# First stage in another order: 1/rms row later, norm of v ahead of its mixing adds, evictions and M6 of u ahead of S3 and A22, identity products before the first weights

## The chip, the cores and the metric

The kernel runs on one core of a Trainium2 chip. The metric is device microseconds (us) of one execution; less is better. Of the engines, PE (TensorE) does matrix products, DVE (VectorE) and ACT (ScalarE) do elementwise work, POOL (GpSimd) does little here, and SP (SyncE) issues nearly all DMAs. Each engine works through its own list of instructions in order; semaphores order the lists among each other. PE's results stand in PSUM banks, all else in SBUF or in HBM.

## What is computed

One decoder block on 1024 tokens of width 1024, in float32. Cut to what matters here:

```
h = rms_norm(x, g)                                   # x * rsqrt(mean(x^2) + eps) * g
rnn_x, rnn_gate, sgu_u, sgu_v, gate_a, gate_b = split(h @ w_in)
y_a = gelu(rnn_gate) * rg_lru(conv4(rnn_x))          # recurrence over the tokens
v   = layer_norm(gelu(sgu_v))                        # over all 1024 columns of v
y_b = gelu(sgu_u) * (tril(w_s) @ v + b_s)            # per chunk of 128 tokens, 8 groups
x  += (sigmoid(gate_a)*(y_a @ w_proj_a) + sigmoid(gate_b)*(y_b @ w_proj_b)) @ w_out
x  += (silu(g) * u) @ w_down,  [g|u] = rms_norm(x) @ w_gate_up
return rms_norm(x)
```

## The kernel before

Every product of two f32 matrices is made of three products of split operands: a value is written as hi + lo, and `mm3` issues hi·hi, hi·lo and lo·hi (lines 97, 98 and 99 in the profile). A split is two instructions: ACT writes hi (L93), then DVE subtracts to get lo (L94). Nearly every operand and every piece of a weight passes through this pair. A piece of a weight is 128x512, a part of an activation operand 128x1024 (`part`).

Only the first stage, about the first 200 us, is touched. It has four steps.

Step 1, `wv0`: the first half of the columns of v. x, already transposed in HBM (`xt`), is loaded by quarters (256 tokens) and split with the gain in it (`x_split`, L450 on ACT, L451 on DVE), and eight tiles of 128 tokens go through 24 products each into PSUM (`pv`). Beside this the untransposed x is loaded (`x_load`, tile `xn` with three buffers), squared and summed on ACT (L454), and 1/rms is computed in a chain of small DVE instructions (`rstd_early`, L382 to L391). `x_rms` then puts it on a diagonal `dg` (L463 ACT, L464 DVE), and `x_row` multiplies that by ones on PE (L473), which gives 1/rms as a row over the tokens. With it `scale_x` scales x in place, for the later products. gelu of v reads PSUM with 1/rms as the scale (`gelu_v0` L486, statistics L530).

Step 2, `wv1`: the other half of the columns, again eight tiles of 24 products. After each tile ACT applies gelu (L611) and DVE takes statistics (L612, L618); `v_norm` computes 1/std (L624, then the chain) and centres (L630, ACT); two tiles later `v_split` makes the split normalized v (`vn`, L636 ACT, L637 DVE) and `v_mix` multiplies it with the mixing weights `ws` (PE L647, L648), copies half the result (ACT L650), adds the other (DVE L651) and stores it to HBM (L652, tensor `mix_d`). In between `sums` and `sum_s4` build S1 to S4 out of the four blocks A11, A12, A21 and A22 of the scaled x, and `part` splits them.

Step 3: `u0` and `u1`, two column blocks of u. They are multiplied by a seven-product scheme (`wino`): M1, M2, M5, M6, M3, M7, M4 of 12 products each, whose left operands are A11, A12, S1, S2, S4, S3 and A22, and whose right operands (b11, b21, t1, t2, b22, t3, t4) are made from a 1 MB piece of a weight by DVE subtractions (L206 to L217) and splits. The two go in turn. M1, M6, M7 and M4 run into one PSUM tile, `p1`, so M6 can start only after M1 has been copied out (`post`, L233 on ACT), and M4 only after M7 has been added in (L243 on DVE). While step 3 starts, `post` is put off: its calls are kept in `postponed` and made after all of S3 and A22. Then the results of u are multiplied with the mixed v, which comes back from HBM (DVE L788, gelu L789 on ACT, DVE L791) and are stored.

Step 4: `r0`, a column block of rnn_x, in the same scheme; its result runs through the convolution (`xc`, L857 on ACT, L859 on DVE) and is split (`xs`), and the gate products `pgt` of PE wait for that. After `r0` the rest of the kernel follows in the same rhythm.

Steps 1, 2 and the start of 3 stand under `manual_schedule`: each engine's list there has the order in which the code is written. Behind it a list scheduler orders instructions by its own costs. The lines that it works on are the same, but what of the first part is left to it can be mixed in anywhere behind.

Of the kernel before, what the change touches and what calls it, by code (L numbers as in the profile page):

```python
# [51 lines left out]
def block_kernel(ctx: ExitStack, tc: tile.TileContext, a: dict, out: bass.AP):  # L52
# [139 lines left out]
    cur, postponed = {"misc": None}, []  # L192
# [29 lines left out]
    def wino(name, ops, c11, c21, c12, c22, c11_dst=None, order=STEADY):  # L222
# [28 lines left out]
        for m in order:  # L251
# [163 lines left out]


# [3 lines left out]
    H = [[slot(f"h{h}{kh}") for kh in range(2)] for h in range(2)]  # L420
    ops = {}
    with tc.tile_pool(name="phv", bufs=1) as wk:
        ws = wk.tile([P, GROUPS, 2, P], F32R, name="ws")
        shift = wk.tile([P, GROUPS, P], F32, name="shift")
# [8 lines left out]
        xn = {}  # L433
        a22 = []
        dgs = {}

        def xt_load(q, ks=slice(0, NK)):
            c = slice(2 * P * (q % 2), 2 * P * (q % 2 + 1))
            nc.sync.dma_start(F[q // 2][:, ks, c], a["xt"][q][:, ks])
# [13 lines left out]
        def squares(t):  # L453
            act.activation(xn[t], xn[t], AF.Square, accum_out=ssqs[:, t:t + 1])  # L454

        def x_rms(q):
# [3 lines left out]
            dg = wk.tile([P, 2, 2, P], F32R, name=f"dg{q}", tag="dg")  # L460
# [4 lines left out]
            dgs[q] = dg  # L465
# [91 lines left out]
        x_load(3)  # L557
        xt_load(3)
        x_load(4)
        x_rms(0)  # L560
        x_split(2)
        for t in range(2, NT):
            acc[t] = ps(f"pv0{t}")
            tm_half(acc[t], "wv0", H, t, range(NK), free=NK * (t == NT - 1))
            if t == 2:
                x_row(0)
# [37 lines left out]
        part("A11", block(0, 0, 1), 1)  # L604
# [755 lines left out]
```

## Time and profile before

| | |
|---|---|
| median of 3 runs | 1451.16 us (1450.82 to 1451.53) |
| profiled execution | 1452.88 us |
| its span from first to last instruction | 1451.2 us |
| mean granted clock of TensorE | 0.990 of full speed |
| PE busy | 1400.2 us, 96% of the span |
| DVE busy | 1098.3 us, 76% |
| ACT busy | 793.5 us, 55% |
| chain that ended last | PE 76%, DVE 11%, ACT 6%, DMA 4%, issue 2% |

The chain is followed back from the last instruction, at each step to what released it, so its shares say on which engine the end hangs. By the page's slices PE has its low ones at the start and around the span's tenth, and from there on it stands at 90% or more until the last slice; the granted clock is below full speed in the first four slices only. The steps in time: wv0 runs to 59 us, wv1 to 129 us, u0 and u1 to about 183 us, and r0 to 205 us.

### The profile page before, as it was taken

The numbers are of one execution on the slowest core, as the hardware profiler recorded it, in microseconds if no ns is written. First come the engines' busy times: TensorE is split into PE (matmuls) and PEld (weight loads), VectorE is DVE, ScalarE is ACT, GpSimd is POOL, SyncE is SP. The second block draws the span as 40 slices with busy tenths as digits, with TensorE's granted clock in tenths as the row PEclk, the third lists the DMA queues.
The fourth block names the chain that finished last, engine by engine and source line by source line (L and its number), as shares of the span: only waits on it lengthen the run. The fifth ranks groups of instructions, "written<-read, shape, count | busy, mean of one in ns | idle before, by whom it ended". The sixth has DMA issues, their size and how long they took to land.

```text
span 1451.2 us, 17181 instructions
## 1 busy us (share of the span) xinstructions
PE 1400.2 (96%) x6192; PEld 1153.3 (79%) x6192; DVE 1098.3 (76%) x1803; ACT 793.5 (55%) x1315; POOL 74.8 (5%) x59
## 2 busy tenths in 40 slices
PE   7998699999999999999999999999999999999997
PEld 5776587788888888778888788888888888888886
DVE  6878889988888878597855966666666665697585
ACT  6456668789888876262443633333333333444454
POOL 0000000000000000000000011111111111100000
PEclk9998899999999999999999999999999999999999
DMA  8412445632233367676531032222222226853342
GB/s 294 157 44 70 157 173 176 206 123 93 78 122 140 117 261 293 234 263 217 188 122 44 22 134 109 109 109 110 105 88 105 103 81 266 312 196 109 109 138 80
DMA packets 72821, 212.45 MB, mean 146 GB/s; under 512 B 6560, under 2 KB 20384, under 8 KB 60192
## 3 DMA queue, kind: packets, MB, share of 16 engines
q1 hardware_dynamic: 72592, 211.32, 40.8%
q8 instruction: 48, 0.79, 0.2%
q14 instruction: 37, 0.30, 0.1%
q10 hardware_dynamic: 144, 0.04, 0.0%
HBM read 148.68 MB, written 62.65 MB: 146 GB/s over the span
## 4 chain that ended last, share of the span: by engine, by line
PE 76%; DVE 11%; ACT 6%; DMA 4%; issue 2%; SPq 0%; DVEq 0%; ACTq 0%; POOL 0%; POOLq 0%
PE f_p L99 10%; PE f_p L97 10%; PE f_p L98 10%; PE d_M L98 5%; PE d_M L97 5%; PE d_M L99 5%; PE g_p L99 3%; PE g_p L98 3%; PE g_p L97 3%; PE r_p L99 2%; DMA sb<-sgb_d 2%; PE r_p L98 2%; PE r_p L97 2%; PE po L97 2%; PE po L99 2%; PE po L98 2%
## 5 line engine op out<-in xcount | busy, mean ns | idle before, releaser
L93 ACT ACTIVATE dl_M<-wraw 128x512 fp32r<-128x512 f32 x77 | 48.6, 631 | 104.8 <-PE d_M L99 89.8
L98 PE MATMUL d_M<-d_M,dl_M 128*128 128x512 f32 x264 | 102.8, 389 | 0.0
L97 PE MATMUL d_M<-d_M,dl_M 128*128 128x512 f32 x264 | 102.7, 389 | 0.0
L99 PE MATMUL d_M<-d_M,dl_M 128*128 128x512 f32 x264 | 102.7, 389 | 0.0
L93 ACT ACTIVATE f_t<-wraw 128x512 fp32r<-128x512 f32 x88 | 55.5, 630 | 83.8 <-PE f_p L99 71.4
L94 DVE TENSOR_TENSOR dl_M<-wraw,dl_M 128x512 fp32r<-128x512 f32 x77 | 54.0, 701 | 51.5 <-ACT dl_M L93 51.3
L94 DVE TENSOR_TENSOR f_t<-wraw,f_t 128x512 fp32r<-128x512 f32 x88 | 71.7, 815 | 23.7 <-ACT f_t L93 22.6
L97 PE MATMUL f_p<-m,f_b 128*128 128x512 f32 x176 | 69.2, 393 | 0.0
L98 PE MATMUL f_p<-m,f_b 128*128 128x512 f32 x176 | 69.0, 392 | 0.0
L99 PE MATMUL f_p<-m,f_b 128*128 128x512 f32 x176 | 69.0, 392 | 0.0
L98 PE MATMUL f_p<-m,f_t 128*128 128x512 f32 x176 | 68.5, 389 | 0.0
L99 PE MATMUL f_p<-f_S,f_t 128*128 128x512 f32 x176 | 68.5, 389 | 0.0
L97 PE MATMUL f_p<-f_S,f_t 128*128 128x512 f32 x176 | 68.5, 389 | 0.0
L99 PE MATMUL f_p<-m,f_t 128*128 128x512 f32 x176 | 68.5, 389 | 0.0
L97 PE MATMUL f_p<-m,f_t 128*128 128x512 f32 x176 | 68.5, 389 | 0.0
L98 PE MATMUL f_p<-f_S,f_t 128*128 128x512 f32 x176 | 68.5, 389 | 0.0
L93 ACT ACTIVATE f_b<-wraw 128x512 fp32r<-128x512 f32 x66 | 41.1, 626 | 36.8 <-PE f_p L99 31.6
L94 DVE TENSOR_TENSOR f_b<-wraw,f_b 128x512 fp32r<-128x512 f32 x66 | 45.3, 687 | 19.6 <-ACT f_b L93 18.9
L97 PE MATMUL pv<-wv,h 128*128 128x512 f32 x128 | 51.5, 403 | 7.8 <-ACT wv L93 7.8
L97 PEld LDWEIGHTS d_M<-d_M,dl_M 128*128 128x128 f32 x264 | 49.6, 188 | 10.4
L98 PEld LDWEIGHTS d_M<-d_M,dl_M 128*128 128x128 f32 x264 | 49.6, 188 | 10.3 <-DVE d_M L94 0.2
L99 PEld LDWEIGHTS d_M<-d_M,dl_M 128*128 128x128 f32 x264 | 49.6, 188 | 10.3
(504 smaller groups left out, 4213.0 us busy)
## 6 DMA issues: line engine op xcount, KB each, us to landing
wraw<-in_w_gu_dram SPq DMA_DIRECT2D x22, 1024.0 KB, 4.8
wd<-in_w_down_dram SPq DMA_DIRECT2D x11, 1024.0 KB, 9.4
wraw<-in_w_r_dram SPq DMA_DIRECT2D x8, 1024.0 KB, 6.1
wraw<-in_w_g_dram SPq DMA_DIRECT2D x8, 1024.0 KB, 4.8
wraw<-ffs_d SPq DMA_DIRECT2D x8, 1024.0 KB, 5.1
wraw<-ffa_d SPq DMA_DIRECT2D x6, 1024.0 KB, 6.1
xn<-in_x_dram SPq DMA_DIRECT2D x8, 512.0 KB, 6.2
wraw<-in_w_u_dram SPq DMA_DIRECT2D x4, 1024.0 KB, 5.3
```

Source lines behind the costliest of these rows:

```text
L93: act.activation(hi, src, AF.Copy)
L94: (eng or dve).tensor_sub(lo, src, hi.bitcast(F32))
L97: pe.matmul(o, lh, rh, start=start, stop=False, **kw)
L98: pe.matmul(o, lh, rl, start=False, stop=False, **kw)
L99: pe.matmul(o, ll, rh, start=False, stop=stop, **kw)
```

## The change

It writes the first stage in another order, and has to house some tiles elsewhere for it.

1. Start: the first 512 KB piece of transposed x is loaded as two of 256 KB (128 tokens each), and its splits are halved with it. Before the first real product PE gets 12 products of the 128x128 f32 identity with itself into a PSUM tile that nobody reads (`warm`).
2. 1/rms: `x_row` of each quarter comes one tile later; the diagonal (`x_diag`) is made after the next quarter's `x_split` instead of before it. The untransposed x has a slot of four tiles (`xn`) instead of three buffers, so its loads are issued earlier. A11 is split in wv1 instead of wv0, since it takes over that slot.
3. Norm of v: `v_norm` runs for the groups 0, 1+2, 3+4, 5+6, 7, right behind the statistics of its last tile. The additions of the mixed tile of two tiles before (`v_mixed`), which stood ahead of the norm, now stand behind it, and the centring (`v_centre`) behind those. S1's split comes one or more tiles later than its sum.
4. u: the PSUM copies and additions (`post`) are no longer put off until after S3 and A22: `take(2)` makes them two at a time in between, and four products of each u (M1, M2, M5, M6) instead of three are written out under `manual_schedule`. S3 and A22 are split after that. A22 is now scaled in place and copied by ACT (two instructions 128x1024, in tiles that the last stores of mixed v must have left) before its split. What the finished results of u trigger (`results`) is still called behind the manual part.

```diff
-    cur, postponed = {"misc": None}, []
+    cur, postponed = {"misc": None, "defer": False}, []
...
-            if cur["misc"] is None:
+            if cur["defer"]:
                 postponed.append(lambda m=m: post(m))
...
+    xn = slot("xn", (P, 4, D), F32)
     ops = {}
+    new_misc("misc1")
...
-            xn[t] = wk.tile([P, D], F32, name=f"xn{t}", tag="xn", bufs=3)
-            nc.sync.dma_start(xn[t], a["x"][ts(t), :])
...
+            nc.sync.dma_start(xn[:, t % 4], a["x"][ts(t), :])
...
             rstd_early(wk, ssqs[:, c], 1.0 / D, f"rx{q}", 2, rms[:, c])
-            dg = wk.tile([P, 2, 2, P], F32R, name=f"dg{q}", tag="dg")
+
+        def x_diag(q):
+
+            dg = dgs[q] = wk.tile([P, 2, 2, P], F32R, name=f"dg{q}", tag="vb", bufs=3)
...
-                y = F[h][:, k]
-                if h == 1 and k >= 4:
-                    if k % 2 == 0:
-                        a22.append(wk.tile([P, 2, HALF], F32, name=f"a22_{k}", tag="xn", bufs=3))
-                    y = a22[-1][:, k % 2]
-                dve.scalar_tensor_tensor(y, F[h][:, k], par("mix_g", k), R[h], ALU.mult, ALU.mult)
+                dve.scalar_tensor_tensor(F[h][:, k], F[h][:, k], par("mix_g", k), R[h], ALU.mult, ALU.mult)
...
-            s1 = wk.tile([P, 2, HALF], F32, name=f"xs{i}", tag="xn", bufs=3)
-            dve.tensor_add(s1, block(1, 0, i), a22[i])
-            part("S1", s1, i)
+            s1 = s1s[i] = wk.tile([P, 2, HALF], F32, name=f"xs{i}", tag="shift")
+            dve.tensor_add(s1, block(1, 0, i), block(1, 1, i))
...
-        xt_load(0, slice(0, 4))
+        first, second = slice(0, P), slice(P, 2 * P)
+        xt_load(0, slice(0, 4), first)
         start_loads(1)
+        xt_load(0, slice(0, 4), second)
         xt_load(0, slice(4, 8))
...
+        warm = ps("warm")
+        for _ in range(12):
+            pe.matmul(warm[:, :P], ident, ident, start=True, stop=True, skip_group_check=True)
...
             if t == 2:
-                x_row(0)
                 v0_done(0, acc[0])
...
             if t == 3:
+                x_row(0)
                 x_split(3)
+                x_diag(1)
...
-                part("A11", block(0, 0, 0), 0)
-                x_rms(3)
                 v0_done(6, acc[6])
             tick()
         x_row(3)
-        part("A11", block(0, 0, 1), 1)
...
+        group = {t: [t] if t in (0, NT - 1) else [t - (t + 1) % 2, t + t % 2] for t in range(NT)}
...
+            if 1 <= t < 3:
+                part("A11", block(0, 0, t - 1), t - 1)
+            if t == 2:
+                sums(0)
+            if t == 4:
+                part("S1", s1s[0], 0)
+                sums(1)
...
             v_stats(t, acc)
-            if t == NT - 1:
+            if t == group[t][-1]:
                 v_norm(t)
             if t > 1:
                 v_mix(t - 2)
-            if t in (1, 3, 5, 6):
-                v_norm(t)
+                v_mixed(t - 2)
+            if t == group[t][-1]:
+                v_centre(t)
             tick()
...
+        def take(n):
+            for fn in postponed[:n]:
+                fn()
+            del postponed[:n]
+
+        cur["defer"] = True
         v_split(6)
         head("u0")
         v_mix(6)
+        v_mixed(6)
         v_split(7)
         head("u1")
-        part("S2", block(0, 0, 0), 0)
+        take(2)
         head("u0")
         v_mix(7)
+        v_mixed(7)
+        part("S2", block(0, 0, 0), 0)
+        head("u1")
         part("S2", block(0, 0, 1), 1)
+        take(2)
+        head("u0")
         head("u1")
         part("S4", block(0, 1, 0), 0)
+        take(2)
+        part("S4", block(0, 1, 1), 1)
         head("u0")
-        part("S4", block(0, 1, 1), 1)
         head("u1")
-        for i in range(2):
-            part("S3", block(1, 0, i), i)
-        for i in range(2):
-            part("A22", a22[i], i)
...
+        take(2)
+        cur["defer"] = False
     ms.__exit__(None, None, None)
...
-        for fn in postponed:
+        for fn in results:
             fn()
-        postponed.clear()
+        results.clear()
+        for i in range(2):
+            part("S3", block(1, 0, i), i)
+        for i in range(2):
+            c = wk.tile([P, 2, HALF], F32, name=f"a22_{i}", tag="rr")
+            act.activation(c, block(1, 1, i), AF.Copy)
+            s1s[i] = c
+        for i in range(2):
+            part("A22", s1s[i], i)
```

The order in which the engines get this stands below at three places.

The first is DVE in wv1: `mv` and `rv` are the norm's tiles (L118 to L129 of the list), `mt` the additions of mixed v, `vn` the splits of normalized v. Before:

```order
L651 TENSOR_TENSOR mt10_849<-mt10_849,mx10_844 128x256
L651 TENSOR_TENSOR mt11_858<-mt11_858,mx11_853 128x256
L651 TENSOR_TENSOR mt12_867<-mt12_867,mx12_862 128x256
L651 TENSOR_TENSOR mt13_876<-mt13_876,mx13_871 128x256
L624 TENSOR_SCALAR mv2_771<-mv2_771 128x2
L382 TENSOR_SCALAR rv3_881<-mv2_771 128x2
L383 TENSOR_SCALAR rv3_881<-rv3_881 128x2
L389 TENSOR_TENSOR rv3_881<-rv3_881 128x2
L390 TENSOR_TENSOR rv3_881<-rv3_881 128x2
L391 SCALAR_TENSOR_TENSOR rv3_881<-rv3_881 128x2
L389 TENSOR_TENSOR rv3_881<-rv3_881 128x2
L390 TENSOR_TENSOR rv3_881<-rv3_881 128x2
```

Now, where the norm of tiles 1 and 2 ends and the additions of tile 0 follow:

```order
L390 TENSOR_TENSOR rv2_789<-rv2_789 128x2
L391 SCALAR_TENSOR_TENSOR rv2_789<-rv2_789 128x2
L389 TENSOR_TENSOR rv2_789<-rv2_789 128x2
L390 TENSOR_TENSOR rv2_789<-rv2_789 128x2
L391 SCALAR_TENSOR_TENSOR rv2_789<-rv2_789 128x2
L687 TENSOR_TENSOR mt00_806<-mt00_806,mx00_801 128x256
L687 TENSOR_TENSOR mt01_813<-mt01_813,mx01_808 128x256
L687 TENSOR_TENSOR mt02_820<-mt02_820,mx02_815 128x256
L687 TENSOR_TENSOR mt03_827<-mt03_827,mx03_822 128x256
L667 SCALAR_TENSOR_TENSOR vn10_866<-va1_366,rv2_789,vn10_866 128x512
L667 SCALAR_TENSOR_TENSOR vn11_869<-vb1_742,rv2_789,vn11_869 128x512
L641 BN_STATS st3_447<-vb3_872 128x6
```

The four `mt` additions of a tile stood ahead of the whole norm; now the norm's last rows are through before they begin, and the split `vn` follows them.

The second is ACT at the copies of M1: `u0_y1` and `u1_y1` are copies of `p1`, `h_S3` and `h_A22` the splits of S3 and A22, `u0_t1` and the like pieces of u's weight. Before:

```order
L93 ACTIVATE h_S4_1415<-x0_129 128x2x512
L93 ACTIVATE u0_t3_1499<-wraw4_615 128x512
L93 ACTIVATE u1_t3_1502<-wraw5_641 128x512
L93 ACTIVATE u0_t4_1520<-wraw4_615 128x512
L93 ACTIVATE h_S3_1453<-x1_130 128x2x512 x2
L93 ACTIVATE u1_t4_1540<-wraw5_641 128x512
L93 ACTIVATE h_A22_1458<-a22_4_710 128x2x512
L93 ACTIVATE h_A22_1458<-a22_6_713 128x2x512
L233 ACTIVATE u0_y1_1471<-u0_p1_1263 128x512
L233 ACTIVATE u1_y1_1473<-u1_p1_1323 128x512
L239 ACTIVATE u0_m5_1495<-u0_p2_1425 128x512
```

Now:

```order
L93 ACTIVATE u0_t1_1336<-wraw4_630 128x512
L233 ACTIVATE u0_y1_1352<-u0_p1_1279 128x512
L233 ACTIVATE u1_y1_1354<-u1_p1_1339 128x512
L93 ACTIVATE u1_t1_1358<-wraw5_656 128x512
L681 ACTIVATE mt70_1379<-mx70_1374 128x256
L681 ACTIVATE mt71_1386<-mx71_1381 128x256
L681 ACTIVATE mt72_1393<-mx72_1388 128x256
L681 ACTIVATE mt73_1400<-mx73_1395 128x256
L93 ACTIVATE h_S2_1410<-x0_129 128x2x512
L93 ACTIVATE u0_b22_1413<-wraw4_630 128x512
L849 ACTIVATE a22_0_1538<-x1_130 128x1024
L93 ACTIVATE u0_t2_1417<-wraw4_630 128x512
```

The two copies L233 stood behind all splits of S4, S3 and A22; now they stand ahead of the last tile's `mt` copies and of the first split of S2. The copy of the first half of A22 (L849) is new and stands ahead of `u0_t2`, which M6 of u0 needs.

The third is DVE up to M6 of u1, which needs `u1_t2`; `u0_y1` and `u1_y1` are the additions of M2, `mix00` and `mix20` the mixed v loaded back. Before:

```order
L94 TENSOR_TENSOR u0_t2_1399<-wraw4_615,u0_t2_1399 128x512
L94 TENSOR_TENSOR h_S4_1415<-x0_129,h_S4_1415 128x2x512
L94 TENSOR_TENSOR u1_b22_1418<-wraw5_641,u1_b22_1418 128x512
L210 TENSOR_TENSOR wraw5_641<-wraw5_641 128x512
L217 TENSOR_TENSOR wraw5_641<-wraw5_641 128x512
L94 TENSOR_TENSOR u1_t2_1422<-wraw5_641,u1_t2_1422 128x512
L94 TENSOR_TENSOR h_S4_1415<-x0_129,h_S4_1415 128x2x512
L94 TENSOR_TENSOR u0_t3_1499<-wraw4_615,u0_t3_1499 128x512
L94 TENSOR_TENSOR u1_t3_1502<-wraw5_641,u1_t3_1502 128x512
L94 TENSOR_TENSOR u0_t4_1520<-wraw4_615,u0_t4_1520 128x512
L94 TENSOR_TENSOR h_S3_1453<-x1_130,h_S3_1453 128x2x512 x2
L94 TENSOR_TENSOR u1_t4_1540<-wraw5_641,u1_t4_1540 128x512
```

Now:

```order
L94 TENSOR_TENSOR u0_t2_1417<-wraw4_630,u0_t2_1417 128x512
L94 TENSOR_TENSOR h_S2_1410<-x0_129,h_S2_1410 128x2x512
L236 TENSOR_TENSOR u0_y1_1352<-u0_y1_1352,u0_p3_1361 128x512
L236 TENSOR_TENSOR u1_y1_1354<-u1_y1_1354,u1_p3_1420 128x512
L94 TENSOR_TENSOR u1_b22_1437<-wraw5_656,u1_b22_1437 128x512
L830 SCALAR_TENSOR_TENSOR mix00_1515<-mix00_1515,pv_119,sh0_1518 128x512
L210 TENSOR_TENSOR wraw5_656<-wraw5_656 128x512
L833 TENSOR_TENSOR u0_y1_1352<-mix00_1515,u0_y1_1352 128x512
L830 SCALAR_TENSOR_TENSOR mix20_1524<-mix20_1524,pv_119,sh1_1527 128x512
L217 TENSOR_TENSOR wraw5_656<-wraw5_656 128x512
L833 TENSOR_TENSOR u1_y1_1354<-mix20_1524,u1_y1_1354 128x512
L94 TENSOR_TENSOR u1_t2_1441<-wraw5_656,u1_t2_1441 128x512
```

Ahead of `u1_t2` there are now two additions of M2 and two rows each of the mixed v (L830 and L833 of the changed code, L788 and L791 before), which read what a DMA brings; S4, `u0_t3`, `u1_t3`, S3 and A22 come behind it.

## Rows read from the trace of the kernel before

**Rows 1.** Page, part 1: busy time, share of the span, instructions.

```profile
PE 1400.2 (96%) x6192; PEld 1153.3 (79%) x6192; DVE 1098.3 (76%) x1803; ACT 793.5 (55%) x1315; POOL 74.8 (5%) x59
```

**Rows 2.** Stretches from:to in us: length, busy time by engine, granted clock, DMA.

```profile
0.00:202.95 202.95, 171.66 (x769) 140.57 (x770) 164.38 (x368) 119.75 (x223) 1.97 (x8) 0.95 0.45 151
110.00:120.00 10.00, 7.00 (x28) 6.15 (x29) 8.14 (x25) 7.24 (x14) 0.00 (x0) 0.66 0.23 65
155.00:165.00 10.00, 3.60 (x9) 2.82 (x10) 7.25 (x9) 5.98 (x10) 0.10 (x1) 0.51 0.81 283
200.00:300.00 100.00, 97.75 (x428) 79.59 (x427) 93.78 (x150) 81.72 (x120) 0.30 (x3) 1.00 0.50 169
```

**Rows 3.** Waits of PE, 0 to 260 us: us in total, times, longest.

```profile
PE u_p L97 <- ACT u_y L233: 11.3, 1, 11.3
PE pv L97 <- ACT wv L93: 7.8, 2, 7.5
```

**Rows 4.** Waits of DVE, 16 to 203 us: us in total, times, longest.

```profile
DVE vn L637 <- ACT vn L636: 4.0, 5, 1.2
DVE st L612 <- ACT vb L611: 3.8, 1, 3.8
DVE h_S L94 <- ACT h_S L93: 3.0, 5, 1.1
DVE rx L382 <- ACT xn L454: 3.0, 2, 1.6
DVE mix L788 <- DMA sh<-shift_d: 2.6, 2, 1.5
DVE dg L464 <- ACT dg L463: 2.2, 4, 0.6
DVE shift L500 <- PE rs L497: 1.4, 1, 1.4
DVE u_t L94 <- ACT u_t L93: 1.3, 1, 1.3
DVE xr L236 <- PE r_p L99: 0.9, 1, 0.9
DVE h_A L94 <- ACT h_A L93: 0.5, 1, 0.5
```

**Rows 5.** Timeline of PE: start, duration; idle before it in brackets.

```profile
33.85 0.77 PE L473 MATMUL rms<-dg,ones 128*128 128x256 f32 x2 [1.79 <-ACT dg L463]
161.40 0.80 PE L97 MATMUL u_p<-h_S,u_t 128*128 128x512 f32 x1 [11.27 <-ACT u_y L233]
204.66 0.39 PE L97 MATMUL pgt<-xs,wg 128*128 128x512 f32 x1
801.93 1.23 PE L400 MATMUL h_t<-ident,hf 128*128 128x128 f32 x8 [0.97 <-DVE hf L1071]
```

**Rows 6.** Timeline of DVE and ACT: second quarter of x, M6, the gate.

```profile
16.11 3.31 ACT L450 ACTIVATE h<-x,pv 128x256 fp32r<-128x256 f32 x8 [1.71 <-DMA x<-in_xt_dram]
160.75 1.08 ACT L233 ACTIVATE u_y<-u_p 128x512 f32<-128x512 f32 x2 [1.48 <-DVE h_A L94]
164.14 0.75 DVE L788 SCALAR_TENSOR_TENSOR mix<-mix,pv,sh 128x512 f32<-128x512 f32 x1 [1.47 <-DMA sh<-shift_d]
200.20 0.68 DVE L243 TENSOR_TENSOR r_m<-r_m,r_p 128x512 f32<-128x512 f32 x1
202.25 0.69 DVE L94 TENSOR_TENSOR xs<-xc,xs 128x512 fp32r<-128x512 f32 x1
```

**Rows 7.** Groups of instructions, DVE, 128.8 to 203 us: busy, mean ns.

```profile
L94 DVE TENSOR_TENSOR u_t<-wraw,u_t 128x512 fp32r<-128x512 f32 x11 | 7.4, 688 | 1.3 <-ACT u_t L93 1.3
```

**Rows 8.** DMA issues: size of each, us to landing.

```profile
mix_d<-mt SPq DMA_DIRECT2D x12, 128.0 KB, 1.9
mix<-mix_d SPq DMA_DIRECT2D x8, 256.0 KB, 3.8
lam<-in_lam_dram SPq DMA_DIRECT2D x1, 4.0 KB, 4.7
```

More of the change, by code (lines that the diff above doesn't have):

```diff
@@ L414, in tm_half, with new_misc, end_misc, u_tile @@
                 inner[k]()
+    def new_misc(name):
+        cur["pool"] = tc.tile_pool(name=name, bufs=1, side="right")
+        cur["misc"] = cur["pool"].__enter__()
+    def end_misc():
+        cur["pool"].__exit__(None, None, None)
+        cur["misc"] = None
+    def u_tile(name, tag="u"):
+        return cur["misc"].tile([P, HALF], F32, name=name, tag=tag, bufs=6 if tag == "u" else 1)
+    def load(dst, src):
+        nc.sync.dma_start(dst, src)
+    def store(dst, src):
+        nc.sync.dma_start(dst, src)
     state["limit"] = NK
@@ L420, in block_kernel @@
     H = [[slot(f"h{h}{kh}") for kh in range(2)] for h in range(2)]
+    xn = slot("xn", (P, 4, D), F32)
     ops = {}
+    new_misc("misc1")
     with tc.tile_pool(name="phv", bufs=1) as wk:
         ws = wk.tile([P, GROUPS, 2, P], F32R, name="ws")
-        shift = wk.tile([P, GROUPS, P], F32, name="shift")
+        shift = wk.tile([P, GROUPS, P], F32, name="shift", tag="shift")
         ones = wk.tile([P, P], F32R, name="ones", tag="vb", bufs=3)
@@ L432, in block_kernel, with xt_load, x_split @@
         R = {}
[L433 to L439, printed above, removed]
+        s1s = {}
+        def xt_load(q, ks=slice(0, NK), c=slice(0, 2 * P)):
+            o = 2 * P * (q % 2)
+            nc.sync.dma_start(F[q // 2][:, ks, o + c.start:o + c.stop], a["xt"][q][:, ks, c])
         def x_load(t):
-            xn[t] = wk.tile([P, D], F32, name=f"xn{t}", tag="xn", bufs=3)
-            nc.sync.dma_start(xn[t], a["x"][ts(t), :])
-        def x_split(q, ks=range(NK)):
-            c = slice(2 * P * (q % 2), 2 * P * (q % 2 + 1))
+            nc.sync.dma_start(xn[:, t % 4], a["x"][ts(t), :])
+        def x_split(q, ks=range(NK), c=slice(0, 2 * P)):
+            c = slice(2 * P * (q % 2) + c.start, 2 * P * (q % 2) + c.stop)
             for k in ks:
@@ L544, in block_kernel @@
         x_load(2)
+        x_load(3)
+        xt_load(3)
         act.activation(ones, ident, AF.Copy, scale=0.0, bias=1.0)
-        for k in range(NK):
+        for k in range(4):
+            x_split(0, (k,), first)
+            pump(k + 1)
+        x_split(0, range(4), second)
+        for k in range(4, NK):
             x_split(0, (k,))
@@ L650, in v_mix, with v_mixed @@
                 act.activation(mt, mx[:, :, 1], AF.Copy)
+                mts[t].append((mt, mx))
+        def v_mixed(t):
+            for i, (mt, mx) in enumerate(mts.pop(t)):
+                g = 2 * i
                 dve.tensor_add(mt, mt, mx[:, :, 0])
@@ L662, in block_kernel @@
                 scale_x(1, range(4 * t, 4 * t + 4))
-            elif 4 <= t < 6:
-                sums(t - 4)
-            elif t >= 6:
-                part("A12", block(0, 1, t - 6), t - 6)
-                sum_s4(t - 6)
+            if 1 <= t < 3:
+                part("A11", block(0, 0, t - 1), t - 1)
+            if t == 2:
+                sums(0)
+            if t == 4:
+                part("S1", s1s[0], 0)
+                sums(1)
+            if t == 5:
+                part("S1", s1s[1], 1)
+                part("A12", block(0, 1, 0), 0)
+            if t == 6:
+                part("A12", block(0, 1, 1), 1)
+                sum_s4(0)
+            if t == 7:
+                sum_s4(1)
             v_stats(t, acc)
-            if t == NT - 1:
+            if t == group[t][-1]:
                 v_norm(t)
```

72 lines of the change are left out of this document (31 added, 41 removed).

## The prediction

> **What bounds the kernel now.** I read the page first: PE is busy 96% of the span and DVE 76% [rows 1], so anything that PE waits for costs time and shorter work on other engines costs nothing by itself. Second, the busy time by stretches. Up to 203 us PE is busy 171.66 of 202.95 us, so 31.3 us of its idle time lie in the one stage that the change touches; from 200 to 300 us it is busy 97.75 of 100 [rows 2]. The reader is to see there how close DVE is: 164.38 of 202.95 us up to the first gate products, and 93.78 of 100 behind it. Third, the waits. PE's greatest is 11.3 us, once, on the copy of M1 (L233 on ACT); 7.5 more are the wait for the first weights [rows 3]. The copy itself takes 0.5 us and starts at 160.75, since it stands behind the splits of S4, S3 and A22 in ACT's list, and those go in step with DVE: the row names DVE's A22 split as what ended ACT's last idle time [rows 6]. Last, DVE's own waits in 16 to 203 us: many kinds of 4.0 us at most each, seven of the ten shown for an ACT row that DVE reads at once [rows 4].
>
> So two engines bound this stage in turn: PE waits for a copy behind DVE's queue, and DVE waits in small pieces for ACT and for PE. To know what the reordering is worth I have to follow DVE's queue to the gate, which is the split of `xs` ahead of the `pgt` products and the addition L243 ahead of M4 of r0.
>
> **The change part by part.** *The M1 copy.* It moves ahead of all splits of S2, S4, S3 and A22. The 11.27 us [rows 5] go from PE at that place. If that were all, PE would be about 11 us earlier; but PE then needs `u1_t2`, t3, S4, S3 and A22 from the same DVE queue, whose length is not changed. What counts is when DVE gets through.
>
> *DVE's waits that go.* From the waits [rows 4], for each kind what I take as gone. `vn` 3.6 of 4.0: with the norm a tile earlier ACT has hi ready when DVE comes. `st` 3.8 of 3.8: DVE waited for gelu of the first wv1 tile, behind PE; the two splits of A11 now fill that place, and PE comes there earlier. `h_S` 2.3 of 3.0: ACT has other rows ahead no longer. `rx` 1.2 of 3.0: the square sums follow loads that no longer wait for a buffer, yet the first quarter stays late, since ACT's eight splits of the second quarter begin at 16.11 on a load [rows 6]. `dg` 1.1 of 2.2: the diagonal comes after other rows. `shift` 1.4, `u_t` 1.3 and the mixed v's wait for its load, 2.6, entirely: the load is issued behind the last store, and nine DVE rows stand between. Four kinds from 0.9 (`xr`) over 0.7 and 0.6 to 0.5 (`h_A`), 2.7 together, go as well. Sum: 3.6 + 3.8 + 2.3 + 1.2 + 1.1 + 1.4 + 1.3 + 2.6 + 2.7 = 20.0 us.
>
> *DVE's work ahead of the gate.* Four rows of u2's weight pieces that stood ahead of the `xs` split now stand behind it: 4 x 0.688 [rows 7] = 2.7 us less. The halved first x piece makes four splits into eight, about 0.15 more each: 0.6 more. The norms are five as before, and the A22 copies are ACT's.
>
> *New waits.* The ACT copy of A22 stands ahead of `u0_t2` and waits for the last stores of mixed v, 1.9 us each; and ACT's first row on `lam`, 4.7 us from issue to landing [rows 8], now stands ahead of `u1_t2`, which M6 of u1 needs. Both lie partly beside the splits that DVE still has to do. Bounds: 0 if both are hidden, 6.6 if neither is. I take 2.0, nearer to 0, because DVE has seven other rows of 0.69 or more there.
>
> *The gate.* The `xs` split ends now at 202.25 + 0.69 = 202.94 [rows 6]. Then: 202.94 - 20.0 - 2.7 + 0.6 + 2.0 = 182.8. L243 of r0 now stands just ahead of it, so M4 of r0 may start at 182.1. A product takes 97.75/428 = 0.228 us at full clock [rows 2]. In the new order three first products of `pgt` and u2 and then the twelve of M4 go: 0.7 + 2.7, to 185.6 with 0.1 for the semaphore.
>
> *PE ahead of the gate.* PE alone would be earlier. Of its 31.3 us idle 7.5 stay at the start; 23.8 could go. Where it idled for long the granted clock fell: 0.66 in 110 to 120 us and 0.51 in 155 to 165, half speed for part of the one and nearly all of the other, against 1.00 later [rows 2]. With 7.00 and 3.60 us busy there that lost 7.00 x 0.34 + 3.60 x 0.49 = 4.1 us. 23.8 + 4.1 - 3 (the first mixing products still wait for their norm) = 25. M4 could then start at 204.66 - 2.7 - 25 = 177 and waits 5 us for DVE. An idle time of that size may put the clock to half again: between 0 and 3.4 us (all fifteen products at half); I take 2. M4 ends at 187.6; before it was through at 204.66, when `pgt` began [rows 5]. The gain is 17.0 us.
>
> *Is it kept?* Behind the gate both engines have gained about the same (DVE 20.1 less the 2.7 of work put off), and from 200 to 300 us both are near full [rows 2]; the order is the same again from there on. I cost the rest at nothing. Were DVE's 2.7 us not hidden, they would show as that much less.
>
> *The start.* The diagonal's 1.79 us wait of PE [rows 5] and a start earlier by up to 2 us (half the first x piece, the clock already up) give PE a lead that it then waits off at DVE: nothing in the sum. The twelve identity products cost by the nearest row, eight f32 products of 128 columns in 1.23 us [rows 5], 1.85 us, or twice that at half clock. They lie in PE's 7.5 us wait for the first weights. Bounds: a gain of 2 if PE bounds, a loss of 1 if the smaller pieces delay the weights; I take 0.
>
> Sum: 1452.88 (profiled execution) - 17.0 = 1435.9. That execution is 1.7 above the median of the runs, 1451.16, so 1434.2, in round numbers 1434.
>
> **The rivals.** (a) *PE-bound*: DVE keeps ahead and all of PE's waits go. For it: 202.95 - 164.38 = 38.6 us of DVE's stretch are idle, and the ledger takes 20.0 of them. Against it: about 12 of the rest lie ahead of 16 us, where the loads rule, and the others are pairs of an ACT and a DVE row that stay pairs. Gain 25: 1451.16 - 25 = 1426.
>
> (b) *Half of the waits come back.* DVE reads an ACT row at once and ACT a DVE row at once; a reorder moves such a pair, and may only move the wait. For it: seven of the ten rows of waits are of this sort [rows 4]. Against it: the rows put in between are of other tiles. Gain 17.0 - 10.0 = 7: 1444.
>
> (c) *Slower: round trips in DVE's queue.* Four rows L830 of mixed v now stand in DVE's list ahead of `u0_t3` and S3, each behind data that is stored to and loaded from HBM. Before, the row of this kind idled 1.47 us for its load and all of DVE with it [rows 6]. A store lands 1.9 us after its issue and a load 3.8 [rows 8], 5.7 a trip; were each of the four to wait a trip of its own, 22.8 us. It decides from 17.0/4 = 4.2 us each. Time: 1451.16 - 17.0 + 22.8 = 1457. Against it: the loads are issued in a row behind the last store and don't wait for each other, and nine DVE rows of 0.69 or more, 6.2 us, stand between the last addition and the first such row; one trip just fits. The Trainium skill, "Perfetto Trace Analysis", section "Tensor Engine Instruction (MATMUL, LD_WEIGHTS)", states that ACT, DVE and GPSIMD are strict FIFO, while PE can pull weight loads ahead. By that rule a DVE row that waits for a DMA holds every split behind it, which is what this rival needs; the trace agrees, with that 1.47 us of an idle DVE.
>
> (d) *It does nothing*: the waits go, but DVE's later stretch gives the gain back. 93.78 of 100 us busy [rows 2] speaks for it, 6 us idle in each 100 against. Time 1451.
>
> **How the numbers follow.** The forecast 0.55 (own range 1430 to 1440: 2.0 less or 4.6 more for the new waits, 2 less or 1.4 more for the clock), (a) 0.15, (b) 0.16, (c) 0.08, (d) 0.06. The range goes from 1426 to 1445: all but (c), (d) and the far side of (a). A difference under 0.2%, 2.9 us, can't be told from none. Faster by more: 0.55 + 0.15 + 0.16 = 0.86; within it 0.05, most of (d); slower 0.09, (c) and the rest of (d).
>
> **What would show it.** In the profile after: no PE wait on L233 over 1 us; the wv1 tiles starting 4 us earlier; M6 of u0 over 20 us earlier than 161.40; a PE wait of about 5 us ahead of `pgt` and M4 of r0, on ACT's `xs` or DVE's L243; the `xs` split at about 182; DVE's waits up to there under 8 us in total. The forecast is wrong if `xs` comes before 178 (then a), after 188 (then b), or if DVE idles on DMAs of mixed v by more than 4 us a row (then c). It is also wrong if `pgt` is 17 us earlier and the end isn't: then the later stretch takes it back (d).

## The result

The changed kernel takes 1435.02 us (median of 4 runs, 1434.66 to 1436.32) against 1451.35 of the kernel before beside it: a ratio of 0.9882 with a 95% interval of 0.9867 to 0.9897, so 16 us faster by the medians. The forecast was 1434 with a range of 1426 to 1445. The profiled execution took 1434.66, its span is 1432.8 (1451.2 before).

First the page after, part 1 and the clock by slices, and below them the clock by slices before:

```profile
PE 1401.0 (98%) x6216; PEld 1153.8 (81%) x6216; DVE 1097.9 (77%) x1807; ACT 796.5 (56%) x1320; POOL 74.7 (5%) x59
...
PEclk9999999999999999999999999999999999999999
```

```profile
PEclk9998899999999999999999999999999999999999
```

PE does the same products as before [rows 1], and 24 records more of the identity products. Its idle time fell from 51.0 us (1451.2 - 1400.2) to 31.8, and 5.5 us of that are not won but filled by the identity products. The slices in which the clock was low before are the fourth and fifth, 109 to 181 us, not the first four as said above under the time before; both stand at 0.9 or more now.

The stretches, read as [rows 2]: length, busy time of PE, PEld, DVE, ACT and POOL, clock, DMA.

```profile
54.00:120.00 66.00, 61.39 (x316) 51.00 (x315) 61.53 (x144) 42.68 (x78) 0.00 (x0) 1.00 0.27 87
120.00:182.40 62.40, 57.41 (x248) 46.78 (x248) 56.92 (x103) 38.36 (x63) 0.10 (x1) 0.95 0.54 176
0.00:182.40 182.40, 171.31 (x788) 140.43 (x789) 159.59 (x366) 120.37 (x225) 1.91 (x8) 0.98 0.50 168
...
115.00:125.00 10.00, 8.71 (x38) 6.97 (x38) 9.60 (x23) 7.29 (x15) 0.00 (x0) 0.83 0.36 106
...
140.00:150.00 10.00, 6.75 (x23) 5.22 (x23) 8.39 (x12) 8.09 (x13) 0.00 (x0) 0.83 0.36 107
```

From 54 to 120 us DVE is now busy 61.53 of 66 us; up to the first gate it has 159.59 busy of 182.40 against 164.38 of 202.95 [rows 2]. It waits less and bounds more. Two clock drops are left in this stage, a mean of 0.83 in 115 to 125 us, where v is mixed, and 0.83 in 140 to 150 us, behind the wait of M6 of u1: each a part at 1.2 GHz and the rest at 2.4.

PE's waits up to 260 us, which answer to [rows 3]:

```profile
PE r_p L97 <- DVE r_m L243: 3.6, 1, 3.6
PE u_p L97 <- ACT u_t L93: 3.2, 1, 3.2
PE mx L679 <- DVE vn L667: 2.3, 4, 1.2
PE mx L678 <- ACT vn L666: 2.2, 2, 1.3
PE pgt L97 <- issue: 1.8, 1, 1.8
```

The 11.3 us on L233 are gone, and the 7.5 on the first weights are filled with the identity products up to the first real product at 6.57 us. Two waits stand at the gates that the prediction spoke of, `pgt` (1.8) and `r_p` on L243 (3.6), but the second is at the next column block, r1, not at r0.

DVE's waits, as [rows 4], up to 190 us:

```profile
DVE mt L687 <- ACT mt L681: 3.0, 2, 1.9
DVE h_S L94 <- ACT h_S L93: 1.9, 4, 0.9
DVE rx L382 <- ACT xn L470: 1.9, 2, 1.6
DVE u_t L94 <- ACT u_t L93: 1.8, 2, 1.4
DVE h L467 <- ACT h L466: 1.2, 1, 1.2
DVE dg L483 <- ACT dg L482: 1.1, 2, 0.6
DVE xc L909 <- ACT xc L907: 1.0, 1, 1.0
DVE vn L667 <- ACT vn L666: 0.4, 2, 0.2
DVE st L544 <- ACT va L501: 0.2, 1, 0.2
```

`vn` went from 4.0 to 0.4, and `st` on the first wv1 tile (3.8), mixed v's load, `shift`, `xr` and `h_A` to nothing (the `st` row shown is of wv0); `mt` grew from 0.8 to 3.0. The wait on `xc`, 1.0, lies behind the gate.

The places themselves, in time. On PE:

```profile
143.37 0.70 PE L97 MATMUL u_p<-h_S,u_t 128*128 128x512 f32 x1 [3.25 <-ACT u_t L93]
182.42 0.47 PE L97 MATMUL pgt<-xs,wg 128*128 128x512 f32 x1 [1.76 <-issue]
185.94 0.39 PE L98 MATMUL pgt<-xs,wg 128*128 128x512 f32 x1
227.21 0.47 PE L97 MATMUL r_p<-h_A,r_t 128*128 128x512 f32 x1 [3.60 <-DVE r_m L243]
```

and on ACT and DVE:

```profile
133.57 1.06 ACT L849 ACTIVATE a<-x 128x1024 f32<-128x1024 f32 x1 [2.54 <-DMA mix_d<-mt]
141.06 0.21 ACT L861 ACTIVATE sp_e<-lam 128x8 f32<-128x8 f32 x1 [1.84 <-DMA lam<-in_lam_dram]
181.69 0.63 ACT L93 ACTIVATE xs<-xc 128x512 fp32r<-128x512 f32 x1 [2.96 <-DVE xc L909]
182.17 0.69 DVE L243 TENSOR_TENSOR r_m<-r_m,r_p 128x512 f32<-128x512 f32 x1
182.77 0.69 DVE L94 TENSOR_TENSOR xs<-xc,xs 128x512 fp32r<-128x512 f32 x1
```

The 143.37 is M6 of u1. The wait ahead of `pgt` is put down to "issue", but ACT's part of the split of `xs` ends 0.1 us ahead of that product, and ACT had stood idle 2.96 us for DVE's `xc`: this wait, too, is for DVE. M4 of r0 is through at 185.94, before at 204.66 [rows 5]. How PE's lead over the kernel before grows, the same product in both traces (before minus after):

```
start of the product after     24.6  42.3  76.7  102.9  128.0  150.3  188.7  228.9  468.4  end
lead, us                        1.4   4.0   6.4    4.1   12.7   21.1   19.4   15.6   16.6  18.5
```

It is won in three steps: the row of 1/rms and the start (4.0), the norm of v (8.6 between 103 and 128 us) and M6 (8.4). 5.5 are handed back at the gates of r0 and r1, and 0.9 of them come back at 230 us, where `pgt` waited 0.8 for `xs` before. The last 1.9 come at 588 and 610 us, where waits of 1.36, 2.06 and 1.57 us before are 0.24, 2.09 and 0.77; the code there is as it was, and why they shrank was not followed.

### The profile page after: what moved, and what is told of

It is laid out like the page before. It is cut to its first block, busy times and chain, and to the rows that moved or that the text cites. A ratio compares the mean times of both kernels' runs of the same rounds, so it can differ in the third digit from the quotient of the medians.

```text
span 1432.8 us, 17238 instructions
## 1 busy us (share of the span) xinstructions
PE 1401.0 (98%) x6216; PEld 1153.8 (81%) x6216; DVE 1097.9 (77%) x1807; ACT 796.5 (56%) x1320; POOL 74.7 (5%) x59
## 4 chain that ended last, share of the span: by engine, by line
PE 78%; DVE 10%; ACT 5%; DMA 5%; issue 2%; SPq 1%; DVEq 0%; ACTq 0%; POOLq 0%; POOL 0%
PE f_p L98 10%; PE f_p L97 10%; PE f_p L99 10%; PE d_M L99 5%; PE d_M L97 5%; PE d_M L98 5%; PE g_p L99 3%; PE g_p L98 3%; PE g_p L97 3%; PE r_p L97 2%; PE r_p L99 2%; PE r_p L98 2%; DMA sb<-sgb_d 2%; PE po L97 2%; PE po L99 2%; PE po L98 2%
## 5 line engine op out<-in xcount | busy, mean ns | idle before, releaser
L93 ACT ACTIVATE f_b<-wraw 128x512 fp32r<-128x512 f32 x66 | 41.2, 627 | 36.5 <-PE f_p L99 31.8
L99 PEld LDWEIGHTS d_M<-d_M,dl_M 128*128 128x128 f32 x264 | 49.6, 188 | 10.3
L206 DVE TENSOR_TENSOR wraw<-wraw 128x512 f32<-128x512 f32 x50 | 53.0, 1061 | 1.0
```

The source lines that it names most:

```text
L93: act.activation(hi, src, AF.Copy)
L99: pe.matmul(o, ll, rh, start=False, stop=stop, **kw)
L206: dve.tensor_sub(b11, b12, b11)
```

## The experiments

Two theories were set against each other. D: the stage ends when DVE gets to L243 and the split of `xs`; a wait that goes from PE alone only becomes a wait at the gates. P: PE's lead is what counts, each part is worth the lead that PE wins there. "Slower" or "faster" below is against the changed kernel, by the ratios to the kernel before (each with its interval), in parts of 1451 us. The profiled execution of each run gives the second number, how far PE is behind or ahead at the product that the changed kernel starts at 468 us, beyond the gates and ahead of the waits near 600 us. It is of one execution each, and the clock is in it: behind the wait at M4 of r1 the clock stayed full in the changed kernel's trace and fell in those of e1, e2, e6, e9, e10 and e11, which puts these six 1.2 to 2.5 us further behind (last section).

```
run                    median    ratio   95% interval       against the changed    PE at 468 us
the changed kernel     1435.02   0.9882  0.9867 to 0.9897    -                      -
e1_start_undone        1434.42   0.9875  0.9859 to 0.9890    1.0 faster             0.6 ahead
e2_norm_undone         1439.88   0.9908  0.9892 to 0.9925    3.8 slower             5.7 behind
e3_u_undone            1438.97   0.9904  0.9888 to 0.9920    3.2 slower             4.2 behind
e4_pool                1452.73   0.9995  0.9984 to 1.0007   16.4 slower            12.7 behind
e5_dve_less            1429.51   0.9832  0.9816 to 0.9848    7.3 faster             4.9 ahead
e6_both_better         1435.98   0.9883  0.9867 to 0.9899    0.1 slower             0.5 behind
e7_all_undone          1446.15   0.9949  0.9934 to 0.9964    9.7 slower            10.9 behind
e8_norm_u_undone       1443.80   0.9937  0.9920 to 0.9953    8.0 slower             8.0 behind
e9_m6_free             1434.05   0.9873  0.9856 to 0.9890    1.3 faster             1.9 ahead
e10_one_chain_less     1432.56   0.9860  0.9840 to 0.9881    3.2 faster             0.8 ahead
e11_row_undone         1440.95   0.9910  0.9891 to 0.9929    4.1 slower             0.1 behind
```

Each interval is some 2 us to either side, so a difference of two such rows under 3 us is not shown by the times alone.

One row of DVE sums up most of them: L243 of r1, which M4 of r1 needs. In the changed kernel it starts at 226.37 us; in e2 3.4 us later, in e3 3.2, in e7 9.9 and in e8 7.0 later, near the 3.8, 3.2, 9.7 and 8.0 us of the times.

**e1_start_undone.**

```diff
-        xt_load(0, slice(0, 4), first)
+        xt_load(0, slice(0, 4))
...
-        for _ in range(12):
-            pe.matmul(warm[:, :P], ident, ident, start=True, stop=True, skip_group_check=True)
```

> The changed kernel with part 1 undone: x's first piece whole (512 KB), no identity products. Theory D (the split of xs and L243 on DVE set the gates, PE waits there 1.76 and 3.60 us): PE loses the 1.8 us it led at 15 us and waits that much less at the gates; time as the changed kernel's, within 0.5 us. Rival P (PE's lead adds up to the end): 1.8 us slower.

No slower, as D had it; by the times alone P's 1.8 us would be just possible. The trace decides: PE is 1.8 us behind the changed kernel at 15 us and 1.6 at 77, but 1.2 ahead at 103. So the lead is worth nothing already at the products that mix v and not, as D said, at the gates, whose waits are as they were (1.82 and 3.59). L243 of r0 and of r1 even come 1.7 us earlier than in the changed kernel, since DVE has four rows fewer.

**e2_norm_undone.**

```diff
-            if t == group[t][-1]:
+            if t == NT - 1:
                 v_norm(t)
+                v_centre(t)
             if t > 1:
                 v_mix(t - 2)
                 v_mixed(t - 2)
-            if t == group[t][-1]:
+            if t in (1, 3, 5, 6):
+                v_norm(t)
                 v_centre(t)
```

> The changed kernel with the norm of v as before: groups 0+1, 2+3, 4+5, 6, 7, the norm behind the mixing adds except for the last tile. Theory D: PE loses the 8.6 us of lead that it won between 103 and 119 us, but 5.4 us of that only shorten its waits at the two gates; DVE loses about 3.6 us of waits on vn; 3 to 4 us slower than the changed kernel. Rival P: 8.6 us slower.

3.8 us slower, 5.7 by the trace (3.3 up to M4 of r1, and 2.4 by the clock behind it): D's 3 to 4 and not P's 8.6. DVE's wait on `vn` is back:

```profile
DVE vn L667 <- ACT vn L666: 3.8, 4, 1.2
```

The gate waits did not shrink, against what D expected (`pgt` 1.8 and `r_p` 3.6 again): PE's later start was not absorbed there, DVE came later by as much.

**e3_u_undone.** The copies and additions of u, `take`, are all called behind S4, S3 and A22, which come into the manual part.

```diff
-        take(2)
+        part("S2", block(0, 0, 0), 0)
         head("u0")
...
         for i in range(2):
             part("A22", s1s[i], i)
+        take(len(postponed))
+        cur["defer"] = False
+        ms.__exit__(None, None, None)
```

> The changed kernel with part 4 undone in its order: three products of each u in the manual part, and the copies and additions of u behind the splits of S4, S3 and A22 again. Theory D: M6 of u0 waits again for the copy of M1, until about 151 us; PE is 8 us later at the gate, of which the 3.6 us wait at the second gate gives back about half; 5 us slower than the changed kernel, 8 at most. Rival P: 8.7 us slower. If the copy were hidden anyway: no slower.

3.2 us slower, less than D's 5. PE's waits show both halves of D, the wait for the copy back at 12.1 us, and of the gates only 0.8 left:

```profile
PE u_p L97 <- ACT u_y L233: 12.1, 1, 12.1
...
PE pgt L97 <- ACT xs L93: 0.8, 1, 0.8
```

So the greatest wait of the kernel before, 11.3 us, is worth 3 to 4 us by itself. The copy was not hidden, but most of the wait for it was time that DVE needed in any case.

**e4_pool.** Rows that only prepare stored operands, from DVE to POOL:

```diff
-                dve.tensor_sub(s, y0, y1)
+                pool.tensor_sub(s, y0, y1)
...
-            dve.tensor_sub(r[:, 0], y1, r[:, 0])
+            pool.tensor_sub(r[:, 0], y1, r[:, 0])
```

> The changed kernel with the subtractions and additions that only prepare stored operands (L802, L805 to L807) on POOL instead of DVE: four DVE rows of 0.6 us fewer ahead of the first gate, six or more fewer up to the second. Theory D: L243 and xs come 2.4 us earlier, both gate waits go: 4 to 5 us faster. Rival P (DVE's length does not matter): no change. Third way: POOL and DVE slow each other down, and DVE's rows get longer than 0.69 us: slower.

The third way: 16 us slower. Two of DVE's rows, 150 to 300 us, of the changed kernel (count, busy, mean ns):

```profile
L94 DVE TENSOR_TENSOR r_t<-wraw,r_t 128x512 fp32r<-128x512 f32 x15 | 10.3, 687 | 0.1
L830 DVE SCALAR_TENSOR_TENSOR mix<-mix,pv,sh 128x512 f32<-128x512 f32 x12 | 8.9, 748 | 0.0
```

Of the kernel with the rows on POOL:

```profile
L94 DVE TENSOR_TENSOR r_t<-wraw,r_t 128x512 fp32r<-128x512 f32 x15 | 13.9, 930 | 0.0
...
L830 DVE SCALAR_TENSOR_TENSOR mix<-mix,pv,sh 128x512 f32<-128x512 f32 x12 | 11.9, 1002 | 0.0
```

These rows take a third longer on average: most keep their 0.68 or 0.75 us, but those that meet a POOL row, of 1.4 to 2.2 us on average by line, last up to 1.78. Others that meet none (`xc`, L909: 753 and 745 ns) are as they were. With 32 rows fewer DVE is busy 1111.5 us in place of 1097.9. The Trainium skill, "SBUF — State Buffer", section "Terms", states that DVE and GpSimd share a pair of ports that one locks for a whole instruction while the other blocks; the longer rows agree. The run is no clean test of D, since work moved and DVE's grew at once, but P's "no change" did not come: with no product touched PE's waits on L243 of the r blocks grew from 4.1 to 10.3 us between 150 and 620 us.

**e5_dve_less.** The same rows of y_b left out instead:

```diff
+                if name == "yb":
+                    store(d["sd"][:, k, 0], y0)
+                    return
                 dve.tensor_sub(s, y0, y1)
```

> The changed kernel without the DVE rows that prepare y_b's stored sums and differences (L802, L805 to L807 for y_b; left out of the computation, the stores go on): 4 rows of 0.6 us less ahead of the first gate and 6 more up to the second, no POOL rows in their place. Theory D: L243 and xs come 2.4 us and then 6 us earlier; the gate waits of 1.76 and 3.60 us go, 4 to 5 us faster than the changed kernel. Rival P (DVE's length does not matter): no change.

7.3 us faster, 4.9 by the trace: D, and P is out. Sixteen rows are left out, four ahead of the first gate and six between the two. Both gate waits are gone from PE's list, which now begins

```profile
PE u_p L97 <- DVE u_m L243: 2.2, 1, 2.2
PE u_p L97 <- ACT u_t L93: 2.0, 1, 2.0
PE mx L679 <- DVE vn L667: 1.9, 3, 1.2
```

No product and nothing ahead of u's results was edited, so what was won is DVE's length. The first line is a new meeting point: M4 of u2, at 203.83 us, waits for DVE now.

**e6_both_better.** M6's wait of 3.25 us hangs on two ACT rows: the A22 copy that waits for a store (133.57, idle 2.54) and the one on `lam` (141.06, idle 1.84). Both were moved, and `lam`'s rows put into wv0:

```diff
+        act.dma_start(lam, a["lam"])
...
             if t == 2:
+                act.activation(sp["e"], lam, AF.Abs)
+                act.activation(sp["e"], sp["e"], AF.Exp, scale=-1.0)
                 v0_done(0, acc[0])
```

> The changed kernel with the two ACT rows that held M6's operand taken from ahead of it: the A22 copies behind S3's split, and lam loaded at the start, its ACT rows ahead of the first gelu and its 20 small DVE rows in wv0, where DVE idles. Theory D: DVE loses 2.3 us of waits and about 2 us of rows ahead of the first gate: 4 us faster than the changed kernel. Rival P: M6's wait of 3.25 us goes and nothing else, 3.3 us faster, the gate waits stay as they are. Against both: the wait moves to the next operand, S4 or t3: no change.

No change. M6's wait is gone, but PE is 6.3 us behind at 103 us. ACT's `Exp` stands between other functions and brings two table loads:

```profile
26.28 1.28 ACT L596 ACT_TABLE_LOAD   x1
...
27.80 1.28 ACT L503 ACT_TABLE_LOAD   x1
```

With them the next squares come later, and the second chain of 1/rms starts at 32.47 us, where it starts at 29.43 in the changed kernel. The 17 small DVE rows then take 39.42 to 42.66 us, and the third chain starts at 42.66, where it was 36.46: 3.0 us of the 6.2 are ACT's, 3.2 DVE's. The 1/rms row and everything behind it is delayed by that. By M6 it is won back, at r0 PE is 1.4 ahead, and beyond r1 nothing is left. DVE had looked idle in wv0 (41.1 us busy of 54), but not at this place: in the changed kernel the third chain follows there without a wait.

**e7_all_undone** and **e8_norm_u_undone** put the edits above, and that of e11, together.

> The changed kernel with parts 1, 2 (row and diagonal), 3 (norm) and 4 (order of u) undone together; what is left is where tiles stand: x in a slot, A11 split in wv1, S1 split later than its sum, A22 scaled in place. Theory D: the parts alone gave 0, 4.9 and 4.0 us; together with the 1/rms row 10 to 12, so 1445 to 1447; the rest of the gain, 4 us and more, is DVE's wait for the first wv1 tile that A11's split fills. Rival: the parts cover for each other, and undone together they give all of the gain back: 1451 to 1453.

> Parts 3 and 4 undone together, the rest as changed. Theory D: DVE comes 4 to 5 us later to the splits that the copy of M1 stands behind, and PE waits for that copy in both; 8 to 9 us slower than the changed kernel, the sum of the two. Rival (the parts cover for each other): 12 us or more slower.

9.7 and 8.0 slower, near D's 10 to 12 and 8 to 9: the norm's and u's parts add up (3.8 + 3.2), and some 7 us of the gain are in what e7 leaves as changed: the slot of x, A11's split in wv1, S1's split later than its sum. DVE's waits of e7 say where:

```profile
DVE vn L659 <- ACT vn L658: 3.8, 4, 1.2
DVE rx L382 <- ACT xn L470: 3.0, 2, 1.6
...
DVE st L633 <- ACT vb L632: 0.7, 1, 0.7
```

`vn` and `rx` are back at 3.8 and 3.0, but `st` on the first wv1 tile is 0.7 where it was 3.8 [rows 4], and `h_S` and `shift` have not come back. In all, DVE waits 20.3 us between 16 us and the end of the split of `xs`, 26.8 in the kernel before and 11.5 in the changed one. So the remainder lies in DVE's waits; which of the edits left brings how much of it is open, since no run undid A11's place or the slot alone.

**e9_m6_free.** As e6, but `lam`'s DVE rows stay where they were and its ACT rows follow the A22 copies:

```diff
+            act.activation(c, block(1, 1, i), AF.Copy)
+            s1s[i] = c
+        act.activation(sp["e"], lam, AF.Abs)
+        act.activation(sp["e"], sp["e"], AF.Exp, scale=-1.0)
+        ms.__exit__(None, None, None)
```

> The changed kernel with the A22 copies behind S3's split, and lam loaded at the start with its two ACT rows behind the A22 copies; DVE's rows on it stay where they were, none is added in wv0. Theory D: M6's wait of 3.25 us goes, DVE loses 2.3 us of waits, both gates come 2.3 us earlier: 2 us faster than the changed kernel. Rival P: 3.3 us faster, with the gate waits as they were. Against both: the wait moves on to S4 or t3: no change.

1.3 us faster, within the intervals. By the trace M4 of r1 starts 4.3 us earlier than in the changed kernel, but behind the same 3.6 us wait the clock fell here, and 1.9 of the 4.3 are left beyond it. Both gate waits are as long as before (1.85 and 3.59), which is P's sign; but D's cause is there too, and larger than expected: DVE's waits up to the split of `xs` fell from 11.5 to 7.4 us, by nearly as much as the gates came earlier. The wait at r1 on PE's timeline of this run:

```profile
222.94 0.76 PE L97 MATMUL r_p<-h_A,r_t 128*128 128x512 f32 x1 [3.59 <-DVE r_m L243]
```

The stretch behind it in this run, with the columns of [rows 2], at a clock of 0.74:

```profile
222.00:234.00 12.00, 11.05 (x37) 8.90 (x38) 9.24 (x16) 9.67 (x16) 0.10 (x1) 0.74 0.18 63
```

and the one behind the same wait in the changed kernel, at 1.00 and with 14 products more:

```profile
227.00:239.00 12.00, 11.79 (x51) 9.59 (x52) 11.25 (x19) 11.92 (x19) 0.10 (x1) 1.00 0.42 145
```

**e10_one_chain_less.** On top of e9, 1/rms of the last two quarters in one chain:

```diff
-            rstd_early(wk, ssqs[:, c], 1.0 / D, f"rx{q}", 2, rms[:, c])
+            if q == 2:
+                return
+            if q == 3:
+                c = slice(4, 8)
+            rstd_early(wk, ssqs[:, c], 1.0 / D, f"rx{q}", 4 if q == 3 else 2, rms[:, c])
```

> As e9_m6_free, and 1/rms of the last two quarters in one chain of 11 small DVE rows instead of two, after the squares of all of them: about 2.1 us of DVE rows less in wv0, before DVE is full. Theory D: DVE is bound from about 46 us on, so the 2.1 us come off both gates: 2 us faster than e9. Rival: the tile that waits for the longer way to its 1/rms holds PE in wv0 or DVE for as long: same as e9 or slower.

3.2 us faster than the changed kernel by the medians. The intervals of the two overlap, so that it beats it is not shown; that it beats the kernel before is. Of the 2.1 us expected over e9, 0.6 show up at 150 us (PE 6.1 ahead of the changed kernel against 5.5), and 0.8 against e9's 1.9 is left beyond the gates: L243 of r1 comes 1.0 us later than in e9 (223.10 and 222.12), and the clock fell twice (below). So the 2 us over e9 that D expected are not there.

**e11_row_undone.**

```diff
+        x_diag(0)
         x_split(2)
-        x_diag(0)
```

> The changed kernel with the 1/rms row and its diagonal at their old places (a tile earlier, ahead of the next split of x). Theory D: PE's wait of 1.79 us comes back and only shortens its waits at the gates; DVE waits about 1 us more for the diagonal: 0 to 1 us slower. Rival P: 1.8 us slower.

Two answers. In the profiled execution, 1435.8 us long, PE waits 3.02 us for the row and has lost 3.7 us of lead at 77 us, and at 468 us it is level: D. The three timed runs took 1440.9 to 1441.3, at a mean clock of 0.990 to 0.991 against 0.995. By an estimate from these means, 0.004 to 0.005 of 1434 us, the clock alone makes some 6 us, enough for their 5; but they have no trace, and where it fell in them, and whether the row's place has to do with it, stays open.

## Why the prediction was right, and where it was not

*What bounds.* Right: DVE's arrival at the gate set the end of the stage (e5), and the removed wait of 11.27 us was not the measure of the gain (e3). Of its signs, M6 of u0 came 24 us earlier (137.24), no wait on L233 was left, and `xs` began at 182.77.

*DVE's ledger.* Predicted 182.8 for the end of `xs`, measured 183.46. Of the 20.0 us of waits taken as gone, most went as listed (`st`, `vn`, `shift`, mixed v, `rx`, `dg`), `h_S` kept 1.9 instead of 0.7. What was not foreseen is `mt`, 0.8 before and 3.0 now: DVE waits for ACT's copies of mixed v in two tiles. The waits up to the gate sum to 11.5 us, 26.8 before, where under 8 was predicted (its own terms leave 26.8 - 20.0 + 2.0 = 8.8). Against that DVE was busy 160.6 us up to there (159.59, and 1.1 behind 182.40), where 164.38 - 2.7 + 0.6 = 162.3 was reckoned. No row is shorter: a row without a wait ahead starts some 0.1 us before the one ahead of it ends (`r_m` above starts at 182.17, `xs` at 182.77, each 0.69 long), and with fewer waits more of them stand so. So the sum came out by luck to 0.7 us: two errors, of waits and of busy time, met.

*New waits.* Predicted 2.0 of at most 6.6; both named causes came: DVE idle 1.36 and 0.26 behind the A22 copy and 0.45 and 0.26 behind `lam`, 2.3 together. The prediction named them as DVE's; what it left out is that PE waits there too, 3.25 us at M6 of u1 with the clock at 0.83, so PE was 21.1 ahead instead of 25.

*The gate.* Mis-sized: 5 us wait and 2 us lost to the clock were predicted, 1.76 and none measured (1.00 in the stretch behind it). M4 of r0 was through at 185.94, predicted 187.6. So the gain at this point was 18.7, not 17.0. That the clock stayed full is how it went in five of the six traces with a wait of 1.76 to 1.88 us at this place; in e10's it fell.

*Is it kept?* The step that failed. It was costed at nothing, since DVE's and PE's leads looked alike. The next gate, M4 of r1, had no wait before and has 3.60 us now. What it waits for is DVE's way from L243 of r0 to L243 of r1, where DVE has hardly a gap (3.0 us of waits in 44). The starts of both rows, in the kernel before (the first of its two is in [rows 6]), in the changed kernel (the first is above) and in e3:

```profile
241.94 0.68 DVE L243 TENSOR_TENSOR r_m<-r_m,r_p 128x512 f32<-128x512 f32 x1
```

```profile
226.37 0.69 DVE L243 TENSOR_TENSOR r_m<-r_m,r_p 128x512 f32<-128x512 f32 x1
```

```profile
187.81 0.68 DVE L243 TENSOR_TENSOR r_m<-r_m,r_p 128x512 f32<-128x512 f32 x1
...
229.56 0.68 DVE L243 TENSOR_TENSOR r_m<-r_m,r_p 128x512 f32<-128x512 f32 x1
```

That is 41.74 us before and 44.20 now, 65 rows in place of 60, and four of the five more are the rows of u2 that were put off behind `xs`. With u's order undone it is 41.75 again (e3), with the norm undone 44.20 (e2). So the 2.7 us put off were due at the next gate. The prediction's sentence on them said what they would cost were they not hidden, "that much less", and 3.8 of PE's lead went there (19.4 to 15.6).

The time came out right because errors of 2 to 4 us met: the gate of r0 was better by 1.7, that of r1 worse by 3.8, and 0.9 at 230 us and 1.9 near 600 us came in that were not forecast and that no run ties to a part of the change. In the profiled executions the gain is 18.2 us (1452.88 to 1434.66) for 17.0 forecast. It is luck, too, that the clock stayed full behind the wait at r1 in this execution (last section).

*The start.* Right in effect (e1). The price of the identity products was wrong: 5.49 us for twelve, where 1.85 or twice that was read off a row of eight. The trace shows 24 records for the 12 products; the eight of [rows 5] (L400) are transposes, eight to a tile of 128 tokens in the code, and have one record each. So the row read was of another kind of instruction.

*The rivals.* (a) would have needed DVE to keep ahead, it did not; (c) did not come: no wait on mixed v's loads at all, its loads at 133.67 landed in time. (b) came in part, as `mt`. (d) came in part, as the wait at r1.

## What to carry to other kernels

A wait on the busiest engine is worth no more than the next engine's queue lets through: walk that queue to the next point where the busy engine must meet it, and then to the one after. Rows that are put off past one such point are due at the next. A busy share over a stretch does not show where there is room for more work: the place itself has to be idle, and what the moved rows bring with them on another engine, such as a table load, counts as well (e6).

## What the runs showed of the hardware

PE waits of the same size were followed by the full clock (1.00, 2.4 GHz) in one run and by a part at 1.2 GHz in another. At M4 of r1 seven traces have a wait of 3.41 to 3.60 us on L243. Over the 6 us behind it the granted clock was 1.00 in the changed kernel, 0.76 in e1, 0.72 in e6 and e11, and 0.53 to 0.55 in e2, e9 and e10; over 12 us it was 1.00 in the changed kernel and 0.74 in e9 (above). At `pgt` of r0 six traces have a wait of 1.76 to 1.88 us: the 6 us behind it were at 1.00 in five and at 0.72 in e10. So a wait of some 2 to 4 us costs its length in some executions and more in others: 9 products fewer in the 6 us of e10, 14 fewer in the 12 us of e9, 2 to 3 us at 0.228 us a product. Each trace is of another kernel, so why it falls in one and not in the other is not shown. Runs of one and the same kernel differ as well: the four of e10 go from 1428.79 to 1436.10, at mean clocks from 0.994 to 0.991. The rows for `pgt` of r0, stretches with the columns of [rows 2], of e9:

```profile
178.00:184.00 6.00, 5.83 (x26) 4.80 (x27) 5.03 (x10) 5.01 (x10) 0.00 (x0) 1.00 0.02 7
```

and of e10, where the same length holds 9 products fewer:

```profile
177.00:183.00 6.00, 5.42 (x17) 4.39 (x18) 4.62 (x8) 3.44 (x7) 0.00 (x0) 0.72 0.09 36
```

The Trainium skill, "TensorE: Matmul & The Clock Gate", section "Part 1: The HAM clock gate", states that the window in which activity is judged runs free and does not start anew with the kernel, so that the moment of the change depends on where in it the first product falls. The pairs above are in keeping with that; no run here shows the window itself.

POOL rows beside DVE rows cost DVE more than they took off it: 32 rows fewer, and 13.6 us more of busy time (e4). A product of two 128x128 f32 matrices has two records in the profile, a transpose of that size one (24 for 12 and 8 for 8, see the start).
